# Sums of squares for three heads and for x1: ScalarE along transposed rows in the place of products with a column of ones

## The chip, the cores and the metric

The kernel runs on one core of a Trainium2 chip. Its time is the device time of one execution in microseconds (us); of several runs the median is taken. The core's engines work side by side, each through a queue of its own in order: TensorE (PE in the profile; PEld is its loading of the stationary operand), VectorE (DVE), ScalarE (ACT), GpSimd (POOL) and SyncE (SP), from whose queue most transfers are issued. An engine waits for others by semaphores.

## The reference

One layer of a decoder trunk on 512 tokens of width 1024, in float32. Cut to what matters here:

```python
h = rmsnorm(x, g_pre_mix)
ca, cb, q, k, v, pu, gl = split_cols(h @ w_in)
y_conv = silu(layernorm(causal_depthwise_conv31(ca * sigmoid(cb)))) @ w_conv_out
o = diff_attention(q, k, v, ...)        # 4 heads; each head's o[512, 128] has its rmsnorm
y_attn = o @ w_attn_out
y_pool = pool_mixer(pu, ...) @ w_pool_out
gates = sigmoid(gl).reshape(B, S, 3, D)
merged = gates[0] * y_conv + gates[1] * y_attn + gates[2] * y_pool
x = x + rmsnorm(merged @ w_out)         # called x1 below
h = rmsnorm(x)
f = square(relu(h @ w_mlp_in)) @ w_mlp_out
x = x + rmsnorm(f)
return x + sigmoid(x @ w_ple_gate) * (p @ w_ple_proj)
```

Each rmsnorm needs, for every token, the sum of the squares over the channels.

## The kernel before

Activations stand transposed: channels on the 128 partitions, the 512 tokens along the row, so a vector of 1024 channels is eight tiles of 128 x 512. A float32 product is made of three products of split operands (high and low part): `mm3`, lines 154 to 156. The weights come in 142 chunks of 512 KB: a transfer into one of three `raw` buffers (SyncE's queue, line 76), a cast on ScalarE to `wh` (line 90), a subtraction on VectorE to `wl` (line 94), both into one of the split slots. A raw buffer is free when the subtraction has read it, a split slot when TensorE's last product with the chunk is done.

The input projection makes the conv channels, queries, keys, values, pool channels and 24 gate tiles (eight for each branch). A gate tile is 24 products into one of the four banks tagged "mm"; ScalarE's tanh (line 693) reads the bank out. The bank rotates: the fifth tile from there takes it again. Between these tiles run, as side streams, the attention (logits, exp, transposes, values, and behind the fourth block of a head its norm), the conv (31 taps, then a norm over channels, lines 598 to 615) and the pools. The conv norm's ScalarE work is a tanh (`csg`, line 612), an affine step (`acc`, line 614) and a split (`ch`, line 149) for each of four channel tiles. Then come the product with w_out, the first MLP product, the squares `t`, their split `sh`/`sl`, the second MLP product, and the last gate.

Sums over channels are sums over partitions. `rstd_steps` (line 206) makes them: for each 128 tokens, the tile of squares is the stationary operand of a product with a column of ones (line 211), so that each token's sum lands on a partition of its own. VectorE scales it (`pec`, line 201), GpSimd raises it to -1/2 (`per`, line 203), and four transposes (line 216) spread it over all partitions again. It is called for x (`ssum`), the four heads (`osq`, made by ScalarE at line 509, beside the copy `o` at line 510), the conv norm (`csq`), the two halves of `msum` and `fsum`, and x1 (`x1sum`, whose squares are summed over the eight channel tiles first, and whose scale is copied to `rB` at line 914).

The order of the instructions on every engine is set, except in a few stretches marked as manual, by a scheduler that plans the whole program when it is built; the loops yield small steps of the side streams against a credit of TensorE time.

Of the kernel before, what the change touches and what calls it, by code (L numbers as in the profile page):

```python
# [11 lines left out]
AF = mybir.ActivationFunctionType  # L12
# [22 lines left out]
P = 128  # L35
S = 512
HALF = 256
D = 1024
KT = 8
NH = 4  # L40
# [71 lines left out]
def block_kernel(ctx: ExitStack, tc: tile.TileContext, xT, pT, wts, pool_w, par, rel_bias, onehot, out):  # L112
    nc = tc.nc
# [20 lines left out]
    def act_tile(name, dt=F32, tag=None, pool=None, n=S):  # L134
        uid[0] += 1
        tag = tag or OWN.get(name, "a")
        return (pool or ap).tile([P, n], dt, tag=tag, name=f"{name}_{uid[0]}", bufs=BUFS.get(tag))

    def bank(tag="mm"):
        uid[0] += 1  # L140
        return ps.tile([P, S], F32, tag=tag, name=f"{tag}_{uid[0]}")

    def small(n, name):
        uid[0] += 1
        return sp.tile([P, n], F32, tag=f"{name}{n}", name=f"{name}_{uid[0]}", bufs=8)

    def mul_split(h, l, src, scale=1.0):

        nc.scalar.activation(out=h, in_=src, func=AF.Copy, scale=scale)  # L149
        nc.vector.scalar_tensor_tensor(out=l, in0=src, scalar=scale, in1=h.bitcast(F32),  # L150
                                       op0=ALU.mult, op1=ALU.subtract)

    def mm3(o, sh, sl, mh, ml, first, last):
        nc.tensor.matmul(out=o, lhsT=sh, rhs=mh, start=first, stop=False)  # L154
        nc.tensor.matmul(out=o, lhsT=sh, rhs=ml, start=False, stop=False)  # L155
        nc.tensor.matmul(out=o, lhsT=sl, rhs=mh, start=False, stop=last)  # L156


    start = ExitStack()
# [23 lines left out]
    ident = cp.tile([P, P], F32, name="ident")  # L183
    make_identity(nc, ident)
    ones_col = cp.tile([P, 1], F32, name="ones_col")
# [12 lines left out]
    def rstd_from(ssq, inv_n, n, name):  # L198

        c = small(n, name + "c")  # L200
        nc.vector.tensor_scalar(out=c, in0=ssq, scalar1=inv_n, scalar2=EPS, op0=ALU.mult, op1=ALU.add)  # L201
        r = small(n, name + "r")
        nc.gpsimd.tensor_tensor(out=r, in0=c, in1=neghalf[:, 0:n], op=ALU.pow)  # L203
        return r

    def rstd_steps(sq, lo, n, inv_n, got, tag="at"):


        b = bank(tag)
        for j in range(n):  # L210
            nc.tensor.matmul(out=b[:, j:j + 1], lhsT=sq[:, lo + j * P:lo + (j + 1) * P], rhs=ones_col,  # L211
                             start=True, stop=True)
        r = rstd_from(b[:, 0:n], inv_n, n, "pe")
        yield
        for j in range(n):
            nc.tensor.transpose(out=b[:, j * P:(j + 1) * P], in_=r[:, j:j + 1].to_broadcast([P, P]), identity=ident)  # L216
        got(b[:, 0:n * P])
# [63 lines left out]
    for kt in range(2):  # L281
        h, l = act_tile("ph", F32R), act_tile("pl", F32R)
# [41 lines left out]
    chunk[0] = 2  # L324
    x_rB = []
    steps = rstd_steps(ssum, 0, 4, 1.0 / D, x_rB.append)
    next(steps)
    project_p(6)
# [5 lines left out]
    for kt in range(KT + 1):  # L334
        if kt < KT:
            nc.vector.tensor_tensor(out=x_t[kt], in0=x_t[kt], in1=x_rB[0], op=ALU.mult)  # L336
        if kt > 0:
            h, l = act_tile("xnh", F32R, "xn", xnp), act_tile("xnl", F32R, "xn", xnp)
# [33 lines left out]
    b = bank("at")  # L372
# [71 lines left out]
    def attention():  # L444
        state = {}
# [52 lines left out]
        def values(i):  # L498
            h, qb = divmod(i, 4)
            if qb == 1:  # L500
                state["ob"] = bank("at")
            ob, at = state["ob"], state["at"]
            q0 = (qb - 1) * P
            for j in range(qb + 1):
                vh, vl = (t[:, h * P:(h + 1) * P] for t in v_hl[j])
                mm3(ob[:, q0:q0 + HALF], vh, vl, at[0][:, j, :], at[1][:, j, :], j == 0, j == qb)
            if qb == 3:
                sq, o = act_tile("osq"), act_tile("o")
                nc.scalar.activation(out=sq, in_=ob, func=AF.Square)
                nc.scalar.copy(out=o, in_=ob)  # L510
                state["o"] = (sq, o)

        def normalize(h):
            sq, o = state["o"]

            def scaled(rB):
                nc.vector.scalar_tensor_tensor(out=o, in0=o, scalar=sub_g, in1=rB, op0=ALU.mult, op1=ALU.mult)
                hl = act_tile("oh", F32R), act_tile("ol", F32R)
                mul_split(*hl, o)
                o_hl[h] = hl  # L520
            state["fin", h] = rstd_steps(sq, 0, 4, 1.0 / P, scaled)
            next(state["fin", h])

        def finish(h):
# [2 lines left out]
        n = 4 * NH  # L527
        for i in range(n + 3):
            h, qb = divmod(i, 4)
# [54 lines left out]
    def conv_norm():  # L584
# [16 lines left out]
        yield 2.5  # L601
        c_rB = []
        steps = rstd_steps(csq, 0, 4, 1.0 / S, c_rB.append)
        next(steps)
        for z in range(WAIT_LN):
# [170 lines left out]
    def bank2():  # L776
        turn2[0] += 1
        return bank(("mm", "at")[turn2[0] % 2])
# [18 lines left out]
    def split_output(src, evac, done):  # L797

        W.limit = chunk[0] + KT + 3
        cs = [next_chunk() for _ in range(N_SIDE)]  # L800
        bs = [bank2() for _ in range(N_SIDE)]
        for kt in range(KT):
            for (wh, wl), b in zip(cs, bs):
                mm3(b, wh[:, kt * P:(kt + 1) * P], wl[:, kt * P:(kt + 1) * P], *src[kt], kt == 0, kt == KT - 1)
        for m in range(N_SIDE):
            evac(m, bs[m], slice(0, S))
        cs = [next_chunk() for _ in range(KT - N_SIDE)]
        bs = [bank2() for _ in range(KT - N_SIDE)]
        paced = None
        with tc.manual_schedule(engines={mybir.EngineType.PE}):  # L810
            for hf in range(2):
                for m in range(KT - N_SIDE):
                    for kt in range(KT):
                        half_mm(bs[m], *cs[m], src, kt, HALVES[hf], paced)
                    evac(m + N_SIDE, bs[m], HALVES[hf])
                paced = Paced(done(0), PACE_OUT)
# [18 lines left out]
    x1sum = act_tile("x1sum", tag="norm")  # L835
# [24 lines left out]
    def side_by_side_halves(src, done):  # L860
        cs = [next_chunk() for _ in range(4)]
        bs = [bank2() for _ in range(4)]
        paced = Paced(done(1), PACE_IN)
        with tc.manual_schedule(engines={mybir.EngineType.PE}):
            for sl in HALVES:
                for kt in range(KT):
                    for c, b in zip(cs, bs):
                        half_mm(b, *c, src, kt, sl, paced)
                    if paced.n >= PACE_IN[1] and W.limit < W.n:
                        W.limit, W.pin = W.n, True  # L870
                        W.upto(min(chunk[0] + W_AHEAD, W.n - 1))
                        W.pin = False
        return bs

    def one_tile(src):
        wh, wl = next_chunk()
        b = bank2()
        for kt in range(KT):
            mm3(b, wh[:, kt * P:(kt + 1) * P], wl[:, kt * P:(kt + 1) * P], *src[kt], kt == 0, kt == KT - 1)
        return b  # L880
# [3 lines left out]
    rB2 = [None]  # L884

    def hidden(b):
        t = act_tile("t")
        nc.vector.scalar_tensor_tensor(out=t, in0=b, scalar=0.0, in1=rB2[0], op0=ALU.max, op1=ALU.mult)
        nc.scalar.activation(out=t, in_=t, func=AF.Square)
        hl = act_tile("sh", F32R), act_tile("sl", F32R)  # L890
        mul_split(*hl, t)
        return hl
# [16 lines left out]
    for quarter in range(4):  # L909
        s_hl = []  # L910
        if quarter == 0:
            bs = side_by_side_halves(xg, mix_done)
            rB2[0] = act_tile("rB")
            for _ in rstd_steps(x1sum, 0, 4, 1.0 / D, lambda b: nc.scalar.copy(out=rB2[0], in_=b)):
                pass
            s_hl = [hidden(b) for b in bs]
            s_hl += [hidden(one_tile(xg)) for _ in range(4)]
        else:
            s_hl = [hidden(one_tile(xg)) for _ in range(8)]
        if quarter < 3:  # L920
            for m in range(KT):
                b = one_tile(s_hl)
                if quarter == 0:
                    nc.scalar.copy(out=f[m], in_=b)
                else:
                    nc.vector.tensor_tensor(out=f[m], in0=f[m], in1=b, op=ALU.add)
        else:
            split_output(s_hl, evac_f, f_done)
# [18 lines left out]
    for m in range(4, KT - 1):  # L947
        b = one_tile(x2)
        finish(m, b, slice(0, S))
    wh, wl = next_chunk()  # L950
    for sl in HALVES:
        b = bank2()
# [115 lines left out]
```

## Time and profile before

| | us |
|---|---|
| median of 3 runs | 838.75 |
| lowest and highest run | 838.01, 840.37 |
| profiled execution | 839.83 |
| its span | 838.1 |
| TensorE busy in it | 830.9 |
| ScalarE busy in it | 348.6 |

The profile is of one execution; its span is the time between its first and last instruction, and the execution's own time has 1.7 us more around it. Busy time counts an engine's instructions; TensorE's overlap each other in the pipeline, so a product of 512 columns is listed with 0.39 us where the next one starts 0.23 us later. In a timeline a row gives the start, the duration, the engine, the line, the tile written and the tiles read, and in brackets the idle time before it with the engine that ended it. The profile leaves out the numbers of tiles and chunks, the order of instructions shows them.

### The profile page before, as it was taken

The page shows a single profiled execution, that of the slowest core. Times are in us where ns is not written, and L with a number is a line of the kernel's source. Part 1 is how long each engine was busy: PE and PEld are TensorE (multiplying, and loading weights), DVE is VectorE, ACT ScalarE, POOL GpSimd, SP SyncE. Part 2 cuts the span into 40 slices and gives each one's busy share as a digit, 9 for nine tenths or more (in the row PEclk, how much of TensorE's full clock was granted, in tenths as well). Part 3 has the DMA queues.
Part 4 walks back from the last instruction along what each step waited for, and adds up shares of the span by engine and source line. Part 5 has one row for each costly group of instructions (what it writes and reads, how often), then busy time and mean ns, then how long its engine had stood idle before and what let it go on. Part 6 is the DMA issues. An engine that isn't in the chain of part 4 may idle for free.

```text
span 838.1 us, 10679 instructions
## 1 busy us (share of the span) xinstructions
PE 830.9 (99%) x4180; PEld 703.6 (84%) x4180; DVE 505.4 (60%) x835; ACT 348.6 (42%) x564; POOL 30.0 (4%) x66
## 2 busy tenths in 40 slices
PE   8999999999999999999999999999999999999998
PEld 7788888888888888888999888888888888889997
DVE  5869669965679985675387631443334434435772
ACT  6734635555452323752446542342233223425341
POOL 2210000010000000000000000000000000000000
PEclk9999999999999999999999999999999999999999
DMA  7463322222222232265203423322223222222311
GB/s 270 152 235 112 113 101 76 79 87 75 76 76 78 99 100 82 95 220 181 76 27 119 158 83 118 101 97 82 98 101 101 100 81 97 100 76 76 127 59 68
DMA packets 27523, 89.11 MB, mean 106 GB/s; under 512 B 3244, under 2 KB 3628, under 8 KB 27472
## 3 DMA queue, kind: packets, MB, share of 16 engines
q1 hardware_dynamic: 26160, 83.95, 29.7%
q0 software_dynamic: 1312, 4.47, 1.6%
q8 instruction: 33, 0.54, 0.3%
q14 instruction: 18, 0.15, 0.1%
HBM read 84.20 MB, written 5.52 MB: 107 GB/s over the span
## 4 chain that ended last, share of the span: by engine, by line
PE 97%; DVE 1%; ACT 0%; DMA 0%; POOL 0%; issue 0%; SPq 0%; ACTq 0%
PE mm L154 21%; PE mm L156 21%; PE mm L155 21%; PE at L154 10%; PE at L155 10%; PE at L156 10%; PE at L211 1%; PE at L457 1%; PE at L455 1%; PE at L488 1%; PE at L216 0%; DMA p<-in_pT_dram 0%; DVE wl L94 0%; POOL per L203 0%; DVE x L336 0%; DVE xnl L150 0%
## 5 line engine op out<-in xcount | busy, mean ns | idle before, releaser
L90 ACT CAST wh<-raw 128x1024 fp32r<-128x1024 f32 (+1 forms) x144 | 148.8, 1038 | 331.2 <-PE mm L155 151.7
L94 DVE TENSOR_TENSOR wl<-raw,wh 128x1024 fp32r<-128x1024 f32 (+1 forms) x144 | 173.3, 1208 | 100.7 <-ACT wh L90 100.3
L156 PE MATMUL mm<-xnh,wl 128*128 128x512 f32 x352 | 137.9, 392 | 0.5 <-DVE wl L94 0.4
L155 PE MATMUL mm<-xnl,wh 128*128 128x512 f32 x352 | 137.6, 391 | 0.0
L154 PE MATMUL mm<-xnh,wh 128*128 128x512 f32 x352 | 137.2, 393 | 0.0
L577 DVE SCALAR_TENSOR_TENSOR acc<-u,par_sb,acc 128x512 f32<-128x512 f32 x116 | 81.3, 742 | 1.2 <-ACT acc L571 1.1
L156 PEld LDWEIGHTS mm<-xnh,wl 128*128 128x128 f32 x352 | 66.1, 188 | 14.6 <-DVE wl L94 1.4
L154 PEld LDWEIGHTS mm<-xnh,wh 128*128 128x128 f32 x352 | 66.1, 188 | 14.2 <-ACT xnh L149 0.9
L155 PEld LDWEIGHTS mm<-xnl,wh 128*128 128x128 f32 x352 | 66.1, 188 | 14.1 <-DVE xnl L150 0.4
L154 PE MATMUL mm<-sh,wh 128*128 128x512 f32 (+1 forms) x152 | 54.4, 358 | 0.0
L155 PE MATMUL mm<-sl,wh 128*128 128x512 f32 (+1 forms) x152 | 54.4, 358 | 0.0
L156 PE MATMUL mm<-sh,wl 128*128 128x512 f32 (+1 forms) x152 | 54.3, 357 | 0.0
L154 PE MATMUL at<-sh,wh 128*128 128x512 f32 (+1 forms) x144 | 53.1, 369 | 0.0
L155 PE MATMUL at<-sl,wh 128*128 128x512 f32 (+1 forms) x144 | 53.0, 368 | 0.0
L156 PE MATMUL at<-sh,wl 128*128 128x512 f32 (+1 forms) x144 | 52.9, 368 | 0.0
L154 PE MATMUL at<-xgh,wh 128*128 128x512 f32 (+1 forms) x144 | 52.8, 367 | 0.0
L155 PE MATMUL at<-xgl,wh 128*128 128x512 f32 (+1 forms) x144 | 52.7, 366 | 0.0
L154 PE MATMUL mm<-xgh,wh 128*128 128x512 f32 (+1 forms) x144 | 52.7, 366 | 0.0
L156 PE MATMUL mm<-xgh,wl 128*128 128x512 f32 (+1 forms) x144 | 52.7, 366 | 0.0
L156 PE MATMUL at<-xgh,wl 128*128 128x512 f32 (+1 forms) x144 | 52.7, 366 | 0.0
L155 PE MATMUL mm<-xgl,wh 128*128 128x512 f32 (+1 forms) x144 | 52.6, 366 | 0.0
L203 POOL TENSOR_TENSOR per<-pec,neghalf 128x4 f32<-128x4 f32 (+1 forms) x11 | 12.3, 1120 | 581.1 <-DVE pec L201 581.1
(251 smaller groups left out, 1537.9 us busy)
## 6 DMA issues: line engine op xcount, KB each, us to landing
raw<-in_wts_dram SPq DMA_DIRECT2D x140, 512.0 KB, 3.2
x<-in_xT_dram SPq DMA_DIRECT2D x16, 256.0 KB, 5.7
proj_d<-proj POOLq DMA_DIRECT2D x8, 256.0 KB, 4.0
proj<-proj_d SPq DMA_DIRECT2D x8, 256.0 KB, 3.9
out_dram<-pg SPq DMA_DIRECT2D x7, 256.0 KB, 2.0
rep_d<-rel_d POOLq DMA_DIRECT2D x4, 320.0 KB, 8.2
raw<-in_wts_dram SPq DMA_DIRECT2D x4, 256.0 KB, 5.2
bias<-rep_d POOLq DMA_DIRECT2D x4, 256.0 KB, 4.1
```

Source lines behind the costliest of these rows:

```text
L90: i = self.nc.scalar.copy(out=wh[:, sl], in_=src)
L94: i = self.nc.vector.tensor_tensor(out=wl[:, sl], in0=src, in1=wh[:, sl].bitcast(F32), op=ALU.subtract)
L154: nc.tensor.matmul(out=o, lhsT=sh, rhs=mh, start=first, stop=False)
L155: nc.tensor.matmul(out=o, lhsT=sh, rhs=ml, start=False, stop=False)
L156: nc.tensor.matmul(out=o, lhsT=sl, rhs=mh, start=False, stop=last)
L203: nc.gpsimd.tensor_tensor(out=r, in0=c, in1=neghalf[:, 0:n], op=ALU.pow)
L211: nc.tensor.matmul(out=b[:, j:j + 1], lhsT=sq[:, lo + j * P:lo + (j + 1) * P], rhs=ones_col, start=True, stop=True)
L455: nc.tensor.matmul(out=lg[m][:, 0:nn], lhsT=q[m][:, cols], rhs=k[m][:, 0:nn], start=True, stop=False)
L457: nc.tensor.matmul(out=lg[m][:, 0:nn], lhsT=ql[m][:, cols], rhs=k[m][:, 0:nn], start=False, stop=True)
L488: nc.tensor.transpose(out=tp[:, j * P:(j + 1) * P], in_=e[:, j * P:(j + 1) * P], identity=ident)
L577: nc.vector.scalar_tensor_tensor(out=t, in0=u[:, k:k + S], scalar=pcol(w0 + k), in1=t, op0=ALU.mult, op1=ALU.add)
```

## The change

`rstd_steps` gets a new argument. Where it is given, for heads 0 to 2 and x1, each block of 128 tokens is transposed by TensorE into the bank, and ScalarE reads the transposed block along its rows, with the square (heads, on `o` itself) or unchanged (x1, on the sum of squares), and adds up each row (`accum_out`). The elementwise result goes to a tile that nobody reads. The bank is one tile, so transposes and sums of one call alternate. The last head, the conv norm and the halves keep the product with ones.

```diff
--- before.py
+++ after.py
@@ -203,14 +203,23 @@
         nc.gpsimd.tensor_tensor(out=r, in0=c, in1=neghalf[:, 0:n], op=ALU.pow)
         return r
 
-    def rstd_steps(sq, lo, n, inv_n, got, tag="at"):
+    def rstd_steps(sq, lo, n, inv_n, got, tag="at", rows=None):
 
 
         b = bank(tag)
-        for j in range(n):
-            nc.tensor.matmul(out=b[:, j:j + 1], lhsT=sq[:, lo + j * P:lo + (j + 1) * P], rhs=ones_col,
-                             start=True, stop=True)
-        r = rstd_from(b[:, 0:n], inv_n, n, "pe")
+        if rows:
+
+            junk, ssq = act_tile("junk"), small(n, "ssq")
+            for j in range(n):
+                cols = slice(j * P, (j + 1) * P)
+                nc.tensor.transpose(out=b[:, cols], in_=sq[:, lo + j * P:lo + (j + 1) * P], identity=ident)
+                nc.scalar.activation(out=junk[:, cols], in_=b[:, cols], func=rows, accum_out=ssq[:, j:j + 1])
+        else:
+            ssq = b[:, 0:n]
+            for j in range(n):
+                nc.tensor.matmul(out=b[:, j:j + 1], lhsT=sq[:, lo + j * P:lo + (j + 1) * P], rhs=ones_col,
+                                 start=True, stop=True)
+        r = rstd_from(ssq, inv_n, n, "pe")
         yield
         for j in range(n):
             nc.tensor.transpose(out=b[:, j * P:(j + 1) * P], in_=r[:, j:j + 1].to_broadcast([P, P]), identity=ident)
@@ -505,8 +514,10 @@
                 vh, vl = (t[:, h * P:(h + 1) * P] for t in v_hl[j])
                 mm3(ob[:, q0:q0 + HALF], vh, vl, at[0][:, j, :], at[1][:, j, :], j == 0, j == qb)
             if qb == 3:
-                sq, o = act_tile("osq"), act_tile("o")
-                nc.scalar.activation(out=sq, in_=ob, func=AF.Square)
+                sq, o = None, act_tile("o")
+                if h + 1 == NH:
+                    sq = act_tile("osq")
+                    nc.scalar.activation(out=sq, in_=ob, func=AF.Square)
                 nc.scalar.copy(out=o, in_=ob)
                 state["o"] = (sq, o)
 
@@ -518,7 +529,7 @@
                 hl = act_tile("oh", F32R), act_tile("ol", F32R)
                 mul_split(*hl, o)
                 o_hl[h] = hl
-            state["fin", h] = rstd_steps(sq, 0, 4, 1.0 / P, scaled)
+            state["fin", h] = rstd_steps(sq or o, 0, 4, 1.0 / P, scaled, rows=None if sq else AF.Square)
             next(state["fin", h])
 
         def finish(h):
@@ -911,7 +922,7 @@
         if quarter == 0:
             bs = side_by_side_halves(xg, mix_done)
             rB2[0] = act_tile("rB")
-            for _ in rstd_steps(x1sum, 0, 4, 1.0 / D, lambda b: nc.scalar.copy(out=rB2[0], in_=b)):
+            for _ in rstd_steps(x1sum, 0, 4, 1.0 / D, lambda b: nc.scalar.copy(out=rB2[0], in_=b), rows=AF.Copy):
                 pass
             s_hl = [hidden(b) for b in bs]
             s_hl += [hidden(one_tile(xg)) for _ in range(4)]
```

New line numbers in the changed kernel: the transposes of the blocks are line 215, the row sums 216, the gates' tanh 704, the conv norm's steps 623 and 625, the copy of `o` 521. The built program orders instructions anew in other places too.

TensorE at the end of head 0, before: the last value products (`at_205`) and behind them the pool branch's y products (`mm_272`).

```order
L154 MATMUL at_205_1312<-at0_214_1355,vh_86_663 128x256
L155 MATMUL at_205_1312<-at1_214_1356,vh_86_663 128x256
L156 MATMUL at_205_1312<-at0_214_1355,vl_87_664 128x256
L155 MATMUL mm_272_1644<-yl_157_1033,wh26_1480 128x512
L156 MATMUL mm_272_1644<-yh_156_1032,wl26_1481 128x512
L154 MATMUL mm_272_1644<-yh_170_1121,wh26_1480 128x512
L155 MATMUL mm_272_1644<-yl_171_1122,wh26_1480 128x512
```

TensorE some 20 rows on, before: the end of the y products, the products with ones (`osq_242`), and the next head's logits.

```order
L154 MATMUL mm_275_1667<-yh_191_1236,wh26_1480 128x512
L155 MATMUL mm_275_1667<-yl_192_1237,wh26_1480 128x512
L156 MATMUL mm_275_1667<-yh_191_1236,wl26_1481 128x512
L211 MATMUL at_244_1520<-ones_col_129,osq_242_1516 128x1 x4
L488 MATMUL at_247_1536<-ident_124,lg_200_1279 128x128
L455 MATMUL at_249_1544<-k_187_1201,q_185_1199 128x512
```

The same place now, with `at_243` the bank of the block transposes and `o_242` the copy of the head's output.

```order
L154 MATMUL at_205_1312<-at0_214_1355,vh_86_663 128x256
L155 MATMUL at_205_1312<-at1_214_1356,vh_86_663 128x256
L156 MATMUL at_205_1312<-at0_214_1355,vl_87_664 128x256
L215 MATMUL at_243_1518<-ident_124,o_242_1516 128x128
L497 MATMUL at_248_1540<-ident_124,lg_200_1279 128x128
L464 MATMUL at_250_1548<-k_187_1201,q_185_1199 128x512
L464 MATMUL at_251_1549<-k_188_1202,q_186_1200 128x512
L466 MATMUL at_250_1548<-k_187_1201,ql_183_1195 128x512
L466 MATMUL at_251_1549<-k_188_1202,ql_184_1196 128x512
L215 MATMUL at_243_1518<-ident_124,o_242_1516 128x128
L154 MATMUL mm_273_1648<-yh_143_954,wh26_1480 128x512
```

The first block's transpose has moved up to the last value product, the second stands behind the next logits, and the y products (`mm_273`) follow it.

ScalarE around one gate of the conv branch, before: gate_461 reads the bank mm_454; ch, csg and acc are the conv norm, wh57 to wh60 casts of weights.

```order
L149 ACTIVATE ch_459_3062<-acc_407_2402 128x512
L693 ACTIVATE gate_461_3069<-mm_454_3026 128x512
L612 ACTIVATE csg_463_3085<-acc_423_2653,ln_half_345 128x512
L90 CAST wh57_3148<-raw57_3146 128x1024
L614 ACTIVATE acc_423_2653<-acc_423_2653,par_sb_96 128x512
L149 ACTIVATE ch_464_3089<-acc_423_2653 128x512
L693 ACTIVATE gate_466_3111<-mm_462_3077 128x512
L693 ACTIVATE gate_468_3144<-mm_467_3119 128x512
L90 CAST wh58_3181<-raw58_3179 128x1024
L693 ACTIVATE gate_470_3177<-mm_469_3152 128x512
L90 CAST wh60_3252<-raw60_3250 128x1024
```

ScalarE around the same gate now, here gate_464 on the bank mm_457.

```order
L90 CAST wh58_3193<-raw58_3191 128x1024
L90 CAST wh60_3264<-raw60_3262 128x1024
L149 ACTIVATE ch_459_3056<-acc_175_1155 128x512
L623 ACTIVATE csg_461_3070<-acc_410_2414,ln_half_345 128x512
L625 ACTIVATE acc_410_2414<-acc_410_2414,par_sb_96 128x512
L90 CAST wh61_3270<-raw61_3268 128x1024
L149 ACTIVATE ch_462_3074<-acc_410_2414 128x512
L90 CAST wh62_3276<-raw62_3274 128x1024
L704 ACTIVATE gate_464_3081<-mm_457_3038 128x512
L623 ACTIVATE csg_466_3097<-acc_426_2665,ln_half_345 128x512
L625 ACTIVATE acc_426_2665<-acc_426_2665,par_sb_96 128x512
```

The gate stood ahead of the casts of wh57, wh58 and wh60; now it stands behind those and wh61 and wh62, among the conv norm's steps.

TensorE where the bank of that gate is taken again, before: the fifth of the tiles mm_454, mm_462, mm_467, mm_469, mm_471.

```order
L154 MATMUL mm_469_3152<-xnh_54_313,wh55_3073 128x512
L155 MATMUL mm_469_3152<-xnl_55_314,wh55_3073 128x512
L156 MATMUL mm_469_3152<-xnh_54_313,wl55_3074 128x512
L154 MATMUL mm_471_3185<-xnh_40_269,wh56_3115 128x512
L155 MATMUL mm_471_3185<-xnl_41_270,wh56_3115 128x512
```

And now, with mm_457, mm_465, mm_470, mm_472, mm_474.

```order
L154 MATMUL mm_472_3164<-xnh_54_313,wh55_3085 128x512
L155 MATMUL mm_472_3164<-xnl_55_314,wh55_3085 128x512
L156 MATMUL mm_472_3164<-xnh_54_313,wl55_3086 128x512
L154 MATMUL mm_474_3197<-xnh_40_269,wh56_3127 128x512
L155 MATMUL mm_474_3197<-xnl_41_270,wh56_3127 128x512
```

TensorE's order is the same here, chunk for chunk: the tile on wh56 takes the bank of the gate.

At x1 the four blocks' transposes alternate with four sums, and the transposes that spread the scale come some 41 full products later on TensorE. In the second MLP product the new order has 6 products between its first one with the first hidden tile and that with the second, 18 up to the third and 36 up to the fourth; before it was 3, 6 and 9.

## Rows read from the trace of the kernel before

**Rows 1.** The page: busy time (part 1), the chain by engine (part 4)
```profile
PE 830.9 (99%) x4180; PEld 703.6 (84%) x4180; DVE 505.4 (60%) x835; ACT 348.6 (42%) x564; POOL 30.0 (4%) x66
...
PE 97%; DVE 1%; ACT 0%; DMA 0%; POOL 0%; issue 0%; SPq 0%; ACTq 0%
```

**Rows 2.** TensorE's waits: for whom, us in all, times, longest
```profile
PE at L192 <- DVE neghalf L188: 1.1, 1, 1.1
```

**Rows 3.** Line 211: ns min/median/max, first and last start
```profile
L211 PE MATMUL at<-ones_col,osq x32: 164/250/250, 170.6 to 261.6; 128*128 128x1 f32 x32
```

**Rows 4.** Timeline of TensorE at head 0's end: start, us, engine, line, out<-in, count
```profile
165.98 0.40 PE L155 MATMUL mm<-yl,wh 128*128 128x512 f32 x1
...
170.60 0.95 PE L211 MATMUL at<-ones_col,osq 128*128 128x1 f32 x8
171.41 0.31 PE L488 MATMUL at<-ident,lg 128*128 128x128 f32 x1
171.48 0.71 PE L455 MATMUL at<-k,q 128*128 128x512 f32 x2
```

**Rows 5.** Timeline of TensorE at x1's squares
```profile
455.84 0.50 PE L211 MATMUL at<-ones_col,x1sum 128*128 128x1 f32 x4
```

**Rows 6.** Timeline of TensorE, four transposes in one go
```profile
19.52 0.65 PE L216 MATMUL at<-ident,per 128*128 128x128 f32 x4 [0.80 <-POOL per L203]
19.92 0.47 PE L154 MATMUL mm<-ph,wh 128*128 128x512 f32 x1
```

**Rows 7.** Timeline of ScalarE before and after head 0's end
```profile
163.21 0.18 ACT L467 ACTIVATION_READ_ACCUMULATOR lg<-lg,nm 128x1 f32 x1
...
164.70 0.58 ACT L693 ACTIVATE gate<-mm 128x512 f32<-128x512 f32 x1
...
166.18 0.60 ACT L509 ACTIVATE osq<-at 128x512 f32<-128x512 f32 x1 [0.39 <-PE at L156]
166.67 0.58 ACT L510 COPY o<-at 128x512 f32<-128x512 f32 x1
...
171.76 0.28 ACT L149 ACTIVATE at<-at 128x128 fp32r<-128x128 f32 x1
```

**Rows 8.** Timeline of ScalarE at the conv gates
```profile
346.50 0.58 ACT L693 ACTIVATE gate<-mm 128x512 f32<-128x512 f32 x1
...
352.94 1.05 ACT L90 CAST wh<-raw 128x1024 fp32r<-128x1024 f32 x1 [0.72 <-PE mm L155]
...
354.39 1.04 ACT L90 CAST wh<-raw 128x1024 fp32r<-128x1024 f32 x1
...
360.78 1.04 ACT L90 CAST wh<-raw 128x1024 fp32r<-128x1024 f32 x1
```

**Rows 9.** Timeline of TensorE at the conv gates
```profile
352.75 0.39 PE L156 MATMUL mm<-xnh,wl 128*128 128x512 f32 x1
```

**Rows 10.** Timeline of VectorE at the conv gates
```profile
355.46 1.23 DVE L94 TENSOR_TENSOR wl<-raw,wh 128x1024 fp32r<-128x1024 f32 x1 [0.20 <-ACT wh L90]
```

**Rows 11.** DMA issues from 356.6 to 357.0: count, KB each, us to landing
```profile
raw<-in_wts_dram SPq DMA_DIRECT2D x1, 512.0 KB, 4.0
```

**Rows 12.** Stretches: us, busy by engine, granted clock, DMA share, GB/s
```profile
5.50:10.50 5.00, 4.97 (x11) 3.66 (x12) 3.08 (x5) 3.63 (x6) 0.00 (x0) 1.00 0.95 339
834.00:836.00 2.00, 0.00 (x0) 0.00 (x0) 0.85 (x2) 0.38 (x1) 0.00 (x0) 1.00 0.00 0
836.50:838.10 1.60, 0.00 (x0) 0.00 (x0) 0.00 (x0) 0.00 (x0) 0.00 (x0) 0.50 0.05 14
```

**Rows 13.** Timeline of ScalarE behind x1's squares
```profile
465.27 0.58 ACT L914 COPY rB<-at 128x512 f32<-128x512 f32 x1
467.26 0.63 ACT L889 ACTIVATE t<-t 128x512 f32<-128x512 f32 x1 [1.40 <-DVE t L888]
...
469.91 0.63 ACT L889 ACTIVATE t<-t 128x512 f32<-128x512 f32 x1 [0.41 <-DVE t L888]
```

**Rows 14.** Timeline of TensorE at the hidden tiles' products
```profile
478.56 0.39 PE L154 MATMUL at<-sh,wh 128*128 128x512 f32 x1
```

## The prediction

> **What bounds the kernel now.** I read the page's first part and its chain of waits first. TensorE is busy for 830.9 of 838.1 us and the chain lies on it for 97% [rows 1]. The list of TensorE's waits, read next, has no entry over 1.1 us, and the longest is one wait at the start [rows 2]. So there are two ways to change the time: fewer or shorter TensorE instructions, or a new wait of TensorE on another engine. ScalarE is at 42%, but TensorE stands still only if a single result comes late, so a mean share says little here. I therefore went on to the timelines at the places where the order of instructions changes, and asked there which result TensorE needs next and what stands before it in ScalarE's queue.
>
> **What is saved on TensorE.** The profile counts 32 passes for the four heads' products with the column of ones [rows 3], so 8 for one head, two for each of its four blocks; x1's squares have four blocks too, so 8 more. The 8 of head 0 take 171.41 - 170.60 = 0.81 us [rows 4]. Of x1's eight, four lie together and take 0.50 us with the end of the last [rows 5]; I price all eight at 0.9. The change replaces three heads and x1: 3 x 0.81 + 0.9 = 3.3 us go. In their place come 16 transposes of 128 x 128. Four in one go take 19.92 - 19.52 = 0.40 us, 0.10 each [rows 6]; a single one took 171.48 - 171.41 = 0.07 [rows 4]. Most of the 16 stand singly, each with a full matmul behind it that starts a little late; I take 0.11, so 16 x 0.11 = 1.8 us come. Saved: 3.3 - 1.8 = **1.5 us** (bounds: 16 x 0.07 = 1.1 gives 2.2 us saved; 16 x 0.15 = 2.4 gives 0.9). This is all that the edit can win: even with the transposes free it would be 3.3 us, 0.4% of the time.
>
> **New wait 1, the first head.** In the order of before, 20 products of the pool branch stand between the last value product of head 0 and its product with ones; the trace has them from 165.98 to 170.60, 0.23 us each [rows 4], and the squares, made by ScalarE in that time, cost TensorE nothing. In the new order the first transpose stands directly behind the last value product, and waits for the copy of o. ScalarE can start that copy where it started the squares, at 166.18 - now the copy is first, since the squares are gone - and it takes 0.58 us [rows 7]. TensorE would be free at 165.98, the copy's result is there at 166.18 + 0.58 = 166.76, and with some 0.05 for the handover and a weight load the wait is about **0.85 us**. Four matmuls on (one transpose, four products of 0.23 us, then the second transpose) a y product needs the bank of a gate. ScalarE has between the copy and that gate one scaling of 384 columns, the sum of the first transpose (no row shows one; the nearest are a 128-column copy with 0.28 us and the reading of an accumulator with 0.18), and one 128-column copy; then the gate, 0.58 [rows 7]. Counted from the copy's end, the scaling at the 0.5 that lies between the squares' start and the copy's: 0.5 + 0.28 + 0.18 + 0.28 + 0.58 = 1.8 us; TensorE gets there after 0.10 + 0.07 + 4 x 0.23 + 0.10 = 1.2 to 1.4. That is a second wait of about **0.4 us** (bounds 0 and 0.8). In heads 1 and 2 some 25 products still stand between, which at 0.23 us are over 5 us against the copy's 0.58: no wait. The alternation itself puts at least five instructions between two transposes, over 1 us against the sum's 0.46. The ScalarE time that the dropped squares free (0.6 us a head) frees an engine that nobody waits for there.
>
> **New wait 2, the conv gates: the term that decides.** A gate tile is 24 products into one of four "mm" banks; ScalarE's tanh reads the bank out, and the fifth tile from there needs it again. In before the tanh of the tile in question (the gate on mm_454 in the order) ran at 346.50 and ended at 347.08 [rows 8], while TensorE ended the tile before the one that takes the bank over at 352.75 + 0.39 = 353.14 [rows 9]: 6 us of slack. In the new order the conv branch's norm comes later on TensorE and its ScalarE work with it, and the same gate stands behind the casts of four weight chunks (wh58, wh60, wh61, wh62 in the order), which it does not need. ScalarE works its queue in order, so the gate cannot end before the last of these has run. When can wh62 run? Its raw chunk needs a free one of three buffers, which DVE frees with the subtraction for wh60. In before wh58's cast ran at 352.94, when TensorE's last product with the chunk of the same slot was done, and wh60's at 354.39 [rows 8]; the subtraction for wh60 ran from 355.46 to 356.69 [rows 10], the load issued behind it landed 4.0 us later [rows 11], at 360.7, and the cast of wh62 started at 360.78 [rows 8]. These steps start from the same event in both kernels and none of them is changed, so I take them as measured. Then the gate ends at 360.78 + 0.95 (1.04 less the 0.1 by which ScalarE's next instruction starts before the end of one, as in [rows 7]) + 0.58 = 362.31, and TensorE goes on at about 362.35: a standstill of 362.35 - 353.14 = **9.2 us**. From below I bound it by ScalarE's own queue, as if every load were there at once: from 352.94 four casts at 0.95, the four conv instructions between them at no less than 0.49 (one of 512 columns to the next, [rows 7]) and the gate 0.58, together 3.8 + 2.0 + 0.58 = 6.4 us, ending at 359.3: 6.2 us of standstill. From above: should the two loads come a microsecond later, 10.2. I take 9.2, as the load chain is read from rows.
>
> **What the standstill does to the clock.** After the program's last product TensorE does nothing from 834 on; the granted clock was 1.00 on the mean up to 836 and 0.50, 1.2 GHz, from 836.5 to the end [rows 12]. The standstill worked out above is more than three times as long as that idle stretch, so TensorE would come back at 1.2 GHz. The price of coming back I read from the start of the program: from 5.5 to 10.5 TensorE was busy nearly throughout and started only 11 products of 512 columns [rows 12], where 0.23 each would be 2.5 us. The record grants 1.00 there as well, so that it is the clock is my reading of the pace, which is about half of the later one, as 1.2 GHz is of 2.4. Price: 5.0 - 2.5 = **2.5 us**; bounds 0 (the clock stays) and 5.0 (an estimate: twice that). The Trainium skill ("TensorE: Matmul & The Clock Gate", section "Part 1: The HAM clock gate") says that the gate takes an idle TensorE to 1.2 GHz and gives 2.4 GHz back only after it has been busy for a while. The trace's end agrees on the fall (0.50 granted); that a standstill in the middle does it no row of before shows, since none of its waits is longer than 1.1 us [rows 2]. By that rule the sum holds the 2.5, without it it does not.
>
> **x1's squares.** Their sum becomes four transposes alternating with four sums on ScalarE, and the transposes that spread rB stand some 41 full products later in TensorE's order, 41 x 0.23 = 9.4 us. In before rB was copied at 465.27 [rows 13] and TensorE began the products on the hidden tiles at 478.56 [rows 14]: 13.3 us, of which 3.9 are left. The first tile's square ran 2.0 us behind the copy and the next tile's at 469.91, 2.65 us later [rows 13]; with the split behind each square the first is ready some 3.3 us after the copy, the third 5.3 us after the first. The new order has 18 products, 4.1 us, between its first product with the first tile and that with the third, so the third comes at 3.3 + 5.3 = 8.6 against 3.9 + 4.1 = 8.0. That would be a wait of 0.6, but a pace of 2.65 holds casts of weights which the new order has partly ahead of rB; I put **0.15 us** for one short wait there; bounds 0 and 3.
>
> **Sum.** From the profiled execution of before, 839.83 us (span 838.1): -1.5 + 0.85 + 0.4 + 9.2 + 2.5 + 0.15 = +11.6, so 851.4. The profiled execution lies 1.1 us above the median of 838.75; on that the changed kernel comes to **850 us** (850.3), 1.3% slower.
>
> **Rivals.**
> 1. Standstill as above, clock unharmed: 850.3 - 2.5 = 848. For it: the records never show a low clock in the middle. Against: the fall behind the last product. Chance 0.17.
> 2. The gate does not decide (ScalarE reaches it before TensorE needs the bank): then -1.5 + 0.85 + 0.4 + 0.15 = -0.1, so 838.7, no change; with the first-head waits hidden too, 837.3. It ends on the other side, not slower. It decides if ScalarE ends the gate by 353.1 us of before's time, 9 us earlier than worked out; against it stands that the cast of wh58, ahead of the gate, cannot begin before 352.9 [rows 8]. It would also be the case if the transposes are dearer than the passes and nothing else happens. Chance 0.07.
> 3. More than 9: x1's delay makes TensorE wait for the hidden tiles, up to 3 us: 853 to 854, and 856 if the clock falls there as well. Against it is the slack that is left by the count above. Chance 0.08.
>
> The forecast has 0.68. A measurement of this kernel can tell about 0.3%, 2.5 us, from no change. Slower by more: forecast, rivals 1 and 3, 0.93, less a little for a forecast that fails in a way not listed: 0.90. Within 0.3%: rival 2 and part of that, 0.07. Faster by more than 2.5 us would need nearly all the passes for nothing: 0.03. The likeliest case's own range is 847 to 853 (6.2 to 10.2 of standstill, part of the clock's bounds); to hold rival 1 with the lower standstill the range starts at 845.5, and at 853.5 it leaves out most of rival 3.
>
> **What would show it.** In the new profile: in the list of TensorE's waits an mm on L154 that waits for a gate (ScalarE, the tanh line) for about 9 us near 353 us, with the cast of wh62 right before that tanh; a granted clock of 0.5 late in this gap and half-pace products behind it; a transpose of the new line waiting 0.8 us for the copy of o near 166 us; no product with ones for osq but one head's 8 passes. The prediction is wrong if TensorE's idle time between 340 and 365 us stays under 5 us, if the products behind the gap run at 0.23 from the first, or if the hidden tiles' products wait for over a microsecond.

## The result and the profile after

The changed kernel takes 850.15 us (median of 4 runs, 849.06 to 850.9), the kernel before 838.84 in the same comparison: a ratio of 1.0131, interval 1.0117 to 1.0145. The profiled execution took 849.06 us with a span of 847.2.

The page of the changed kernel, TensorE's busy time and the chain by engine:

```profile
PE 830.8 (98%) x4164; PEld 700.7 (83%) x4164; DVE 504.8 (60%) x835; ACT 351.6 (42%) x593; POOL 28.1 (3%) x66
...
PE 95%; DMA 2%; DVE 1%; ACT 1%; SPq 0%; issue 0%; DVEq 0%; ACTq 0%
```

Beside [rows 1], TensorE has as much busy time as before in a span 9.1 us longer, and the chain now crosses transfers and ScalarE. What it waits for is in the list of its waits (engine, tile, line; us in total, times, longest):

```profile
PE mm L154 <- ACT gate L704: 9.0, 1, 9.0
PE at L192 <- DVE neghalf L188: 1.1, 1, 1.1
PE at L215 <- ACT o L521: 0.7, 1, 0.7
```

One wait of 9.0 us on one gate is new, and one of 0.7 at head 0; the second row is that of [rows 2]. The timeline of TensorE behind the long wait:

```profile
360.92 0.80 PE L154 MATMUL mm<-xnh,wh 128*128 128x512 f32 x1 [9.00 <-ACT gate L704]
361.52 0.63 PE L155 MATMUL mm<-xnl,wh 128*128 128x512 f32 x1
361.94 0.63 PE L156 MATMUL mm<-xnh,wl 128*128 128x512 f32 x1
...
363.65 0.53 PE L154 MATMUL mm<-xnh,wh 128*128 128x512 f32 x1
364.01 0.40 PE L155 MATMUL mm<-xnl,wh 128*128 128x512 f32 x1
364.24 0.40 PE L156 MATMUL mm<-xnh,wl 128*128 128x512 f32 x1
```

Behind the first product, starts lie 0.43 us apart up to 363.65 and 0.23 from 364.01 on. The stretches there (us, busy time by engine, granted clock, DMA share, GB/s) show why:

```profile
352.00:354.00 2.00, 0.00 (x0) 0.00 (x0) 1.61 (x3) 2.00 (x3) 0.00 (x0) 1.00 0.00 0
...
358.00:360.00 2.00, 0.00 (x0) 0.00 (x0) 1.68 (x2) 1.50 (x3) 0.00 (x0) 0.50 0.29 119
...
362.00:364.00 2.00, 2.00 (x6) 1.59 (x5) 0.85 (x2) 1.65 (x3) 0.00 (x0) 0.52 0.65 231
364.00:366.00 2.00, 2.00 (x10) 1.66 (x9) 1.67 (x2) 1.80 (x4) 0.00 (x0) 1.00 0.17 68
```

The granted clock fell from 1.00 to 0.50 (from 2.4 to 1.2 GHz) while TensorE stood still, was 0.50 for its first products, and rose at about 364. On ScalarE's side the same time reads so:

```profile
351.73 1.99 ACT L90 CAST wh<-raw 128x1024 fp32r<-128x1024 f32 x2
353.63 0.63 ACT L149 ACTIVATE ch<-acc 128x512 fp32r<-128x512 f32 x1
...
357.25 1.04 ACT L90 CAST wh<-raw 128x1024 fp32r<-128x1024 f32 x1 [1.44 <-DMA raw<-in_wts_dram]
358.20 0.63 ACT L149 ACTIVATE ch<-acc 128x512 fp32r<-128x512 f32 x1
359.33 1.04 ACT L90 CAST wh<-raw 128x1024 fp32r<-128x1024 f32 x1 [0.50 <-DMA raw<-in_wts_dram]
360.28 0.59 ACT L704 ACTIVATE gate<-mm 128x512 f32<-128x512 f32 x1
```

The two rows that wait for a transfer are the casts of wh61 and wh62; ScalarE itself idles ahead of them, with a gate behind them whose input was ready long before. In [rows 8] the same tanh ran at 346.50.

To see where the 9 us lie, I take one event that both traces have, the start of TensorE's last product on a weight chunk (its number from the order of instructions), and subtract:

```
chunk   before   after    after - before   what lies in the step
25      163.54   162.15   -1.39            start of the program, not touched by the change
48      312.26   310.98   -1.28            three heads: +0.11
55      352.75   351.54   -1.21            conv norm: +0.07
56      358.19   367.66   +9.47            the standstill and what follows it: +10.68
69      431.60   441.08   +9.48            nothing
85      522.66   531.81   +9.15            x1: -0.33
141     833.70   842.80   +9.10            nothing
```

The whole loss is made between chunks 55 and 56: 9.00 us of standstill and 1.68 of slow products. The heads came out at nothing, x1 as a small gain; the -1.39 at the start differs from one execution to the next (in the ten other traces below it lies between -1.9 and +0.7).

### The profile page after: what moved, and what is told of

Its sections match the earlier page's. It is cut to its first block, busy times and chain, and to the rows that moved or that the text cites. A ratio compares the mean times of both kernels' runs of the same rounds, so it can differ in the third digit from the quotient of the medians.

```text
span 847.2 us, 10667 instructions
## 1 busy us (share of the span) xinstructions
PE 830.8 (98%) x4164; PEld 700.7 (83%) x4164; DVE 504.8 (60%) x835; ACT 351.6 (42%) x593; POOL 28.1 (3%) x66
## 4 chain that ended last, share of the span: by engine, by line
PE 95%; DMA 2%; DVE 1%; ACT 1%; SPq 0%; issue 0%; DVEq 0%; ACTq 0%
PE mm L156 21%; PE mm L154 21%; PE mm L155 21%; PE at L154 10%; PE at L156 10%; PE at L155 10%; DMA raw<-in_wts_dram 1%; DMA x<-in_xT_dram 1%; PE at L464 1%; PE at L466 1%; PE at L497 1%; ACT wh L90 0%; DVE wl L94 0%; PE at L225 0%; PE at L220 0%
## 5 line engine op out<-in xcount | busy, mean ns | idle before, releaser
L899 DVE SCALAR_TENSOR_TENSOR t<-at,rB 128x512 f32<-128x512 f32 x16 | 11.0, 690 | 38.2 <-PE at L156 34.5
```

## Experiments

Theory: the gate behind the casts is the loss, and it stands there because head 2's norm came late. Rival A: transposes and row sums cost time wherever they stand.

**Heads alone, x1 alone, two heads.** Three kernels do a part of the change.

```diff
-            for _ in rstd_steps(x1sum, 0, 4, 1.0 / D, lambda b: nc.scalar.copy(out=rB2[0], in_=b), rows=AF.Copy):
+            for _ in rstd_steps(x1sum, 0, 4, 1.0 / D, lambda b: nc.scalar.copy(out=rB2[0], in_=b)):
```

> Heads 0 to 2 as in the changed kernel, x1's squares as before. My theory: the loss is the standstill of 9.0 us at the conv gates with the half-pace products behind it, and both come from the heads, so the time stays with the changed kernel: 850.2 (849 to 851.5), the standstill 9 us again. Rival A (the transposes and row sums cost TensorE and ScalarE time wherever they stand, the standstill is only where it shows): x1's four are a quarter of sixteen, so about 847.5.

Measured: 850.36 us, ratio 1.0135 (1.0121 to 1.0148). Its list of TensorE's waits:

```profile
PE mm L154 <- ACT gate L704: 9.4, 1, 9.4
```

The loss is the heads'.

```diff
-                sq, o = None, act_tile("o")
-                if h + 1 == NH:
-                    sq = act_tile("osq")
-                    nc.scalar.activation(out=sq, in_=ob, func=AF.Square)
+                sq, o = act_tile("osq"), act_tile("o")
+                nc.scalar.activation(out=sq, in_=ob, func=AF.Square)
```

> Only x1's squares by transposes and row sums, the heads as before. My theory: no standstill over 1 us, eight passes of 0.9 us go and four transposes of 0.11 come, a short wait for the later rB at most: 838.3 (837.6 to 839.2). Rival A: a quarter of the loss, 841.7. Rival B (the later rB makes TensorE wait for the hidden tiles): 839.5 to 841.5 with a wait on the square of t or its split.

Measured: 838.85, ratio 1.0001 (0.9992 to 1.0010), half a microsecond above the expected centre and no different from before. By the step over chunks 69 to 85 of the traces it gains 0.23 us, which the runs cannot tell. Past the start of the program its list has one wait of TensorE, 0.4 us for a `wl`, and none on the hidden tiles, so rival B fell; the quarter of the loss that rival A gives x1 (841.7) did not come either.

```diff
-                if h + 1 == NH:
+                if h not in (0, 1):
```

and x1 as before:

> Heads 0 and 1 by transposes and row sums, head 2 and x1 as before. My theory: the link from the heads to the conv gates is head 2. Its four transposes stand singly between other products, each waits for the sum before it, so its scale comes 7 us later, and the third conv accumulator stands behind head 2's split in ScalarE's queue (244.42 before, 251.43 after); so the conv norm and its ScalarE work come late. Without head 2's edit the gate stands ahead of the casts again, no standstill there; the waits of 0.7 and some 0.3 at head 0 stay, against 2 x 0.81 - 8 x 0.11 = 0.7 saved: 839.1 (838.3 to 840.2). Rival A: two heads of three, 846.

Measured: 838.89, ratio 1.0004 (0.9995 to 1.0012). Two of three heads cost nothing: no gate is in its list of waits, and what is left of the change there is

```profile
PE at L215 <- ACT o L521: 0.7, 1, 0.7
```

**Head 2 alone.** x1 as before, and in the line of the heads:

```diff
-                if h + 1 == NH:
+                if h not in (2,):
```

> Head 2 alone by transposes and row sums, heads 0 and 1 and x1 as before. My theory: head 2 alone makes the conv norm late. In this order the gate on the bank that TensorE needs next stands behind the casts of wh57 to wh60, not wh61 and wh62, so the standstill is about 5; some 1.5 us more of short waits at head 2 itself, where the first transposes now stand directly behind the last value product; with the half-pace products 846.5 (845 to 848). Rival A (each head a third of the loss): 842.5 without a standstill at the gates.

Measured: 845.9, ratio 1.0087 (1.0074 to 1.0100). The gate:

```profile
PE mm L154 <- ACT gate L704: 5.2, 2, 5.1
```

One head makes a standstill of 5.1 us, as its place behind wh60 and not wh62 lets expect. Of the 1.5 us of short waits expected at head 2 itself the list shows 0.2. The rest is mostly hidden: the profile models a product's end 0.39 us behind its start, where the next one can start after 0.23, so the first 0.16 us of a wait do not show as idle time. By the step over chunks 25 to 48 of the traces this kernel loses 0.89 us although one head's passes save some 0.3, so about 1.2 us of waits came. Rival A, with a third of the loss for a head, is out: heads 0 and 1 cost 0.0004 of the time, which is within the noise, head 2 0.0087.

**The link from head 2 to the gates.** In the timeline of VectorE, head 2's sums (`pec`) and the scaling of its output (`o`), before:

```profile
236.59 0.15 DVE L201 TENSOR_SCALAR pec<-at 128x4 f32<-128x4 f32 x1
...
242.62 0.75 DVE L517 SCALAR_TENSOR_TENSOR o<-o,sub_g,at 128x512 f32<-128x512 f32 x1
```

and in the changed kernel:

```profile
244.16 0.16 DVE L201 TENSOR_SCALAR pec<-ssq 128x4 f32<-128x4 f32 x1
249.23 0.75 DVE L528 SCALAR_TENSOR_TENSOR o<-o,sub_g,at 128x512 f32<-128x512 f32 x1 [4.92 <-PE at L225]
```

The sums are 7.6 us later, though the trace of after is 1.4 us ahead, and VectorE stands 4.9 us. ScalarE has head 2's split (`oh`), a gate, and the third conv tile's accumulator (`acc`) in a row; before:

```profile
243.41 0.63 ACT L149 ACTIVATE oh<-o 128x512 fp32r<-128x512 f32 x1 [0.37 <-DVE o L517]
243.94 0.58 ACT L693 ACTIVATE gate<-mm 128x512 f32<-128x512 f32 x1
244.42 0.81 ACT L571 ACTIVATE acc<-u,par_sb 128x512 f32<-128x512 f32 x1
```

and after:

```profile
250.42 0.62 ACT L149 ACTIVATE oh<-o 128x512 fp32r<-128x512 f32 x1
250.95 0.58 ACT L704 ACTIVATE gate<-mm 128x512 f32<-128x512 f32 x1
251.43 0.80 ACT L582 ACTIVATE acc<-u,par_sb 128x512 f32<-128x512 f32 x1
```

The accumulator starts 7.0 us later, and the third conv tile's 29 taps on VectorE hang on it, with the fourth's behind them and the conv norm behind both. The products that sum the conv norm's squares (`csq`) come 10.6 us later on TensorE; before, they start from 327.3 on:

```profile
L211 PE MATMUL at<-ones_col,csq x8: 164/250/250, 327.3 to 328.0; 128*128 128x1 f32 x8
```

and in the changed kernel from 337.9 on:

```profile
L220 PE MATMUL at<-ones_col,csq x8: 164/250/250, 337.9 to 338.6; 128*128 128x1 f32 x8
```

Head 2's sums are late because its four transposes stand far apart in TensorE's order, each behind the sum before it:

```profile
233.36 0.27 PE L215 MATMUL at<-ident,o 128*128 128x128 f32 x1
238.29 0.27 PE L215 MATMUL at<-ident,o 128*128 128x128 f32 x1
241.97 0.27 PE L215 MATMUL at<-ident,o 128*128 128x128 f32 x1
```

The first is at 227.60. Two kernels test both halves of this link. In the first the transposes need not wait:

```diff
                 nc.tensor.transpose(out=b[:, cols], in_=sq[:, lo + j * P:lo + (j + 1) * P], identity=ident)
+            for j in range(n):
+                cols = slice(j * P, (j + 1) * P)
                 nc.scalar.activation(out=junk[:, cols], in_=b[:, cols], func=rows, accum_out=ssq[:, j:j + 1])
```

> All of the change, but each call traces its four transposes first and its four row sums behind them, so that no transpose waits for a sum; the same instructions in number. My theory: the alternation, not the work, makes head 2's scale late. The transposes stand together, the scale comes as early as before, the gate stands ahead of the casts, no standstill at the conv gates. At head 0 the wait for the copy of o stays (0.7) and the gate behind four sums instead of one costs some 1.5: 840 (838.8 to 841.5). Rival A (the work itself costs it): 849 to 851. Rival C (row sums on ScalarE delay the casts in any order): a standstill of several us stays, 844 to 848.

Measured: 838.61, ratio 1.0002 (0.9993 to 1.0011), 0.2 us below the range that was expected. TensorE's timeline at head 2:

```profile
228.44 0.60 PE L215 MATMUL at<-ident,o 128*128 128x128 f32 x4
```

the third conv tile's accumulator on ScalarE, where before has 244.42 and the changed kernel 251.43:

```profile
243.20 0.81 ACT L584 ACTIVATE acc<-u,par_sb 128x512 f32<-128x512 f32 x1
```

and the waits of this kernel that concern the change:

```profile
PE mm L154 <- ACT gate L706: 0.9, 1, 0.9
...
PE at L215 <- ACT o L523: 0.7, 1, 0.7
```

All the work of the change, in the same number of instructions on TensorE and ScalarE, costs nothing in sum: by the steps of the traces the heads lose 0.67 us (chunks 25 to 48) and x1 gains 0.46 (69 to 85). The remaining gate wait is the one at head 0, 0.9 where 1.5 was expected. Rival C, by which the row sums delay the casts in any order, is out. In the second kernel the squares are not touched at all, and the conv alone is made late:

```diff
     def conv(ct, u):
+        if ct == 2:
+            for z in range(2):
+                yield 0.67
         acc = act_tile("acc")
```

> The kernel before, squares and sums untouched; only the third conv tile's first step is traced two small steps later, so its accumulator stands ten rows later in ScalarE's queue. My theory: the late conv norm alone makes the loss, whatever made it late: the scale's transposes of the conv norm wait some 1.7 us, and the gate stands behind the casts of wh57 to wh63 and waits 13 us; with the half-pace products 854 to 856. Rival A (the sums on ScalarE are the cost): no change, 838 to 840.

Measured: 855.89, ratio 1.0205 (1.0189 to 1.0220), with the waits

```profile
PE mm L154 <- ACT gate L696: 12.2, 1, 12.2
PE at L216 <- POOL per L203: 2.3, 1, 2.3
```

A late conv is enough for the loss, whatever makes it late; here it is later still than in the changed kernel (the `csq` products start at 350.7), and the loss is larger.

**How far back the gate stands.** Three kernels are the changed one with casts kept behind the gate on ScalarE: wh62 alone, wh61 and wh62, and wh57 to wh62. The edit (here the third; the bounds are 62 and 61 in the others; `gates[2]` is the tanh of the gate in question, and the dependency sets an order on one engine without a wait):

```diff
             i = self.nc.scalar.copy(out=wh[:, sl], in_=src)
+            if 57 <= c <= 62:
+                self.tc.add_manual_dep(i.ins, self.gates[2].ins.name, NOSYNC, reason="behind the gate")
...
-        nc.scalar.activation(out=g, in_=b, func=AF.Tanh, scale=0.5)
+        i = nc.scalar.activation(out=g, in_=b, func=AF.Tanh, scale=0.5)
+        if what == "conv gates":
+            W.gates.append(i)
```

> The changed kernel; only the cast of wh62 is kept behind the tanh gate_464 on ScalarE. My theory: the gate then follows the split ch at 358.73 of the changed kernel's profile instead of the cast of wh62, so it ends at 359.3 and the standstill is 7.5 instead of 9.0; the clock still falls: 848.6 (847.8 to 849.6). Rival D (the gate's place does not set the standstill, the late weights do): 850, standstill 9.

> The changed kernel; the casts of wh61 and wh62 are kept behind the tanh gate_464. My theory: the gate follows the conv norm's third split, without a wait for a load: standstill about 5.9 and a short wait of 0.3 at the next gate; 847.2 (846.2 to 848.2) if the clock falls as before. If such a standstill does not lower the clock, 1.5 less, 845.7. Rival D: 850.

> The changed kernel; the casts of wh57 to wh62 are all kept behind the tanh gate_464. My theory: only the late conv norm's steps stand ahead of the gate now: standstill about 3.5 and 0.3 at the next gate. With the fall of the clock 845 (844 to 846), without it 843.4 (842.5 to 844.2), which tells whether an idle stretch of 3.5 us costs the half-pace products too. Rival D: 850.

Measured: 848.45, ratio 1.0117 (1.0098 to 1.0136); 845.79, 1.0086 (1.0069 to 1.0103); 843.75, 1.0055 (1.0037 to 1.0073). Their standstills, in this order:

```profile
PE mm L158 <- ACT gate L708: 7.6, 1, 7.6
```

```profile
PE mm L158 <- ACT gate L708: 5.8, 1, 5.8
```

```profile
PE mm L158 <- ACT gate L708: 3.4, 1, 3.4
```

Against 9.0 in the changed kernel and 7.5, 5.9 and 3.5 expected: the standstill is set by what stands ahead of the gate, cast by cast, and rival D is out. The last of them also splits the price. Its stretches across the standstill, the last one behind it:

```profile
351.60:353.50 1.90, 0.00 (x0) 0.00 (x0) 1.04 (x2) 1.43 (x2) 0.00 (x0) 1.00 0.00 0
353.50:355.00 1.50, 0.01 (x1) 0.01 (x1) 0.81 (x2) 1.18 (x3) 0.00 (x0) 1.00 0.00 0
355.00:357.00 2.00, 2.00 (x9) 1.63 (x10) 0.56 (x2) 2.00 (x3) 0.00 (x0) 1.00 0.03 8
```

The clock stayed at 2.4 GHz, and products ran 0.23 us apart at once; from chunk 55 to 56 this kernel lost 3.74 us, of which 3.40 is the standstill. That is one execution, the shortest of four: 841.86 us at a mean granted clock of 0.999. The other three took 843.52 to 844.67 at 0.995 to 0.997; they were not traced, so the clock may have fallen in them here or at the start of the program, and that a standstill of 3.4 us never brings it down is not shown. In the kernel with wh61 and wh62 kept back the same step lost 7.49, 1.67 above its 5.82 us of standstill, and the clock had fallen:

```profile
354.00:356.00 2.00, 0.00 (x0) 0.00 (x0) 1.93 (x4) 1.86 (x3) 0.00 (x0) 0.50 0.43 147
```

**A version meant to beat both.** From the kernel with the sums behind: head 0 as before, and a head's norm traced a step of the attention later.

```diff
-                if h + 1 == NH:
+                if h not in (1, 2):
...
+            if i > 6 and (i - 4) % 4 == 3:
+                normalize((i - 4) // 4)
+                yield 0.3
...
-                if (i - 3) % 4 == 3:
-                    normalize((i - 3) // 4)
-                    yield 0.3
...
+        normalize(NH - 1)
+        yield 0.3
```

> A version meant to beat both: heads 1 and 2 and x1 by transposes, head 0 as before; the four sums stand behind the four transposes, and a head's norm is traced one step of the attention later, so that other products stand between the copy of o and the first transpose. My theory: no wait at the heads and none at the gates, only the saving of two heads at some 0.4 us each and x1 at 0.4: 837.5 (836.9 to 838.2), 1.1 below the kernel before. Rival E (the short waits only move): 838.6 to 840.

Measured: 837.13, ratio 0.9985 (0.9976 to 0.9994); one of its twelve runs took 2140.62 us, for a reason that no run shows, and is not in the ratio. It is the fastest of all, 1.6 us or 0.15% below the kernel before, where the saved passes promised 1.1; rival E is out. Of its waits only 0.4 us for a `wl`, which the kernel before has too, lies beyond the start of the program:

```profile
PE at L192 <- DVE neghalf L188: 1.1, 1, 1.1
PE mm L156 <- DVE wl L94: 0.6, 2, 0.4
```

## Why the prediction was right, step by step

The time (850 against 850.15) and the mechanism came out; the single terms did so less closely. That the medians agree to 0.15 us is in part luck: in the profiled executions the changed kernel lost 10.5 us from chunk 25 on, where the sum had 11.6, and the price of the clock, its most uncertain term, differs from one profile to the next (1.68 and 2.8 us below).

- **Saved passes**, 1.5 us: measured alone for x1 only, below. A single transpose between two products costs 0.12 here, close to the 0.11 taken:

```profile
205.81 0.27 PE L215 MATMUL at<-ident,o 128*128 128x128 f32 x1
205.84 0.48 PE L154 MATMUL mm<-xnh,wh 128*128 128x512 f32 x1
...
206.39 0.39 PE L156 MATMUL mm<-xnh,wl 128*128 128x512 f32 x1
```

  From 205.81 to 206.39 are 0.58 us, two products and the transpose, less 2 x 0.23.
- **Head 0**, 0.85 and 0.4: the list has 0.7 for the copy of o, counted from a modelled end. By starts the wait is what was forecast: the last value product starts at 163.58, where the next one is usually 0.12 behind, and the transpose

```profile
164.54 0.33 PE L215 MATMUL at<-ident,o 128*128 128x128 f32 x1 [0.68 <-ACT o L521]
...
165.76 0.27 PE L215 MATMUL at<-ident,o 128*128 128x128 f32 x1
165.99 0.50 PE L154 MATMUL mm<-yh,wh 128*128 128x512 f32 x1
```

  is 0.96 behind, 0.84 lost. The second wait is too short for the list: the y product starts 0.23 behind its transpose, against 0.03 in the rows above, so 0.2 of the 0.4 came. That it waits for the gate fits ScalarE's gates from 165.33 on, but the profile names no releaser. For the three heads together the sum had 1.25 lost against some 1.1 saved, +0.15; measured +0.11. These rows account for it: 24 passes gone save 2.43 (3 x 0.81), 12 transposes at 0.12 cost 1.44, and the two waits cost 1.04, together +0.05.
- **The gates**, 9.2: 9.0 in the profile, 9.4 in the kernel with the heads alone. The chain of the loads from [rows 10, 11] held to the cast of wh62 (359.33, or 360.54 in before's time with the 1.21 by which the trace is ahead, against 360.78), and the kernels with casts kept back show that each cast counts.
- **The clock**, 2.5: this term was too large in the profiled execution, 1.68, as 7 products ran slowly and not 11. The price varies: with the heads alone 12 products ran slowly, and the step over chunk 56 was 12.17 us against 9.36 of standstill, 2.8 more. The forecast read the half pace at the start of the program as the clock, against a recorded 1.00. The trace of the kernel with heads 0 and 1 bears it out: there the granted clock is 0.50 from 8.2 to 11.4 us, and products start 0.43 us apart as in before. The forecast's reason for the fall, a standstill longer than the idle stretch at the program's end (under 2.5 us from 834 on), was right for 9 us but is no rule: in one profile the clock stayed at 1.00 through 3.4 us. The Trainium skill ("TensorE: Matmul & The Clock Gate", section "Part 1: The HAM clock gate") says that an idle TensorE falls to 1.2 GHz and gets 2.4 GHz back only after it has been busy for a while; the trace agrees, with 0.50 granted from 358 to 360 and 1.00 again only from 364 on, after 7 products.
- **x1**, -0.4 and +0.15: -0.33, and -0.23 in the kernel with x1 alone. The list has no wait on the hidden tiles; the narrow 0.6 that the count of tiles gave was not there.
- The prediction took the late conv norm from the order of instructions and did not say why it was late. The runs name head 2's alternating transposes.

Rival 1 needed a clock that stays, and it fell in the profiled execution. Rival 2 would have been right for this edit written with its sums behind the transposes. Rival 3 did not show.

## What to carry to other kernels

An edit of 16 small instructions was worth between nothing and 1.6 us by itself (the two versions without a standstill at the gates, 838.61 and 837.13 us); the order that it set off cost eleven. Where a planner orders a whole program, read what stands ahead of each instruction that frees a buffer of the busiest engine, above all work that waits for a transfer. Where a transpose and its reader share one tile, issue all the transposes first: alternating, each waits for the reader, and the last result is late by everything the planner puts between.

## What the runs showed of the hardware that was not expected

The price of a standstill is more than its length. In the one profile with a standstill of 3.4 us the granted clock was 1.00 throughout and the next products ran 0.23 us apart; in the profiles with 5.1, 5.8, 7.6, 9.0, 9.4 and 12.2 us it had fallen to 0.50 when work came back. How long it then stayed at 1.2 GHz did not follow the length: 6 or 7 products after 5.1, 5.8 and 9.0 us, 12 or 13 after 7.6, 9.4 and 12.2. So a standstill that brought the clock down cost 1.6 to 2.8 us on top here, by chance as far as these runs show. The Trainium skill ("TensorE: Matmul & The Clock Gate", section "Part 1: The HAM clock gate") says that the chip judges TensorE's activity by a clock of its own, which does not start with the kernel's work, so that the moment of the rise varies from run to run; 7 slow products after 9.0 us and 12 after 9.4 agree with that, though no run here tests it.
